# High and low meta columns side by side (288, 256 and 272 columns), with drawn places and orders for five weight tiles at a time

## The chip, the cores and the metric

The kernel runs on one core of a Trainium2 chip, in one launch. The metric is the device time of that core in microseconds. Before the change two runs gave 2329.08 and 2329.9 us, median 2329.49 us; the execution that was profiled took 2329.64 us.

## The reference

Two layers of an encoder over 272 positions (256 tokens and 16 learned meta tokens) of width 2048, float32. Cut to what matters:

```python
h = concatenate([meta, x])                       # (272, 2048)
for l in range(2):
    proj = h @ w_in[l]                           # 2048 -> 6176: GLA q,k,v,gate,decay; NA q,k,v
    y = concatenate([gla_mixer(...), na_mixer(...)])
    h = layer_norm(ALPHA * h + y @ w_out[l])     # 2048 -> 2048
    ff = square(relu(h @ w_ff1[l])) @ w_ff2[l]   # 2048 -> 8192 -> 2048
    h = layer_norm(ALPHA * h + ff)
return h[16:]                                    # the meta tokens are dropped
```

Nearly all the work is in the products with `w_in`, `w_out`, `w_ff1` and `w_ff2`, each weight read once from memory. In the second layer most outputs are needed for the 256 tokens alone.

## The kernel before

**Three products for one.** Activations lie transposed: a chunk is 128 features (partitions) by `n` positions, `n` = 272 (`L`) where the meta tokens are needed, 256 (`T`) where not. Every float32 operand is split into a high part in the TensorE's float32r type and the remainder, also float32r (`split`, `halves`). A product of float32 operands is then three float32r products: high weights by high activations ("h"), high weights by low activations ("l"), low weights by high activations ("w"). Each of them loads its 128x128 block of weights first.

**Weight tiles.** `order` lists the tiles of 128x1024 weights (8 blocks of 128 columns) in the order in which they are used, and names each one's kind. `weights` keeps two tiles made ahead: `made` issues the load of `raw` on SyncE's queue, ScalarE casts it to `wh` (L217), VectorE subtracts to get `wl` (L218). Three buffers of each rotate. The tables `HIGHS` and `LOWS` say, by kind, where in `wh` and `wl` the blocks lie: the first element, the step from an even block to the next, and the step from pair to pair, in elements of 4 bytes. Kind "all" has (0, 128, 256) and (0, 144, 320).

**Products.** `by_m` makes one output column block at a time. For each of its tiles `eight` (L252) issues 24 products in the order of `TURNS[False]`, `hlhlww` four times: two blocks by high and low activations, then their low weights. All 24 add into the same `n` columns of one PSUM bank. `by_k` (L303) makes four or eight outputs at once while activations are still being produced, with the same six products per pair of blocks. Where `n` is 256, "h" and "l" become one product of 512 columns (`once`), which needs the high and low parts as one operand; its partial sums are added in `whole`. In the second layer `sixteen` (L264) does this with all high weights of two tiles in one row and all low weights in another. Four PSUM banks ("mm") rotate between outputs. Two extra columns (274 and 258 in place of 272 and 256) carry a layer norm's gain and bias through the first products after it (`fixed`, `fix`).

**Where the parts of an activation lie.** `Pair` holds a chunk's buffer of two rows of 288 elements (2304 bytes in a partition): the high part starts at element 0, the low part at element 288. After a product an evictor (`ev_q`, `ev_f` and so on) reads the bank, and what is used as an activation again goes through `split`: a copy on ScalarE (L338) and a subtraction on VectorE (L339).

The order of the work between the products is set by generators that `pump` steps between tiles, and within an engine's queue by the order in which a scheduler lays the instructions down.

Of the kernel before, what the change touches and what calls it, by code (L numbers as in the profile page):

```python
# [2 lines left out]

# [11 lines left out]
P = 128  # L15
# [25 lines left out]
WIDE = 1280  # L41
HIGHS = {"once": (0, P, 2 * P), "two": (0, P, 2 * P), "all": (0, P, 2 * P), "all2": (0, P, 2 * P), "own2": (0, P + 48, 2 * P + 64)}
LOWS = {"once": (16, P + 32, 2 * P + 64), "two": (16, P + 16, 2 * P + 64), "all": (0, P + 16, 2 * P + 64),
        "all2": (0, P + 48, 2 * P + 64), "own2": (0, P + 32, 2 * P + 64)}
# [12 lines left out]


class Trunk:
    def __init__(self, ctx, tc, ins, out):  # L60
# [5 lines left out]
        self.stream, self.ready = self.order(), deque()  # L66
# [88 lines left out]
    def order(self):  # L155

        i, first = self.i, [(), (WB // 2, WB)]
        for l in range(DEPTH):
            last = l + 1 == DEPTH
            kind = lambda short, name: name if last and short else "all"  # L160
            na = [kind(c % 3 == 0, "two") for c in range(24)]
            groups = [(i["win"][l, g], [kind(g in (3, 4, 5), "two")] * 4 if g < 6 else na[4 * g - 24:4 * g - 20]) for g in range(12)]
# [17 lines left out]
    def weights(self):  # L180

        while len(self.ready) < 2:
            self.ready.append(self.made(*next(self.stream, (None, (), None))))
        return self.ready.popleft()

    def made(self, ap, ends, kind):
        if ap is None:
            return None
# [3 lines left out]
        wh, wl = self.blocks(wh, *HIGHS[kind]), self.blocks(wl, *LOWS[kind])  # L192
# [27 lines left out]
    def head(self, ap, raw, wh, wl):  # L220
# [7 lines left out]
        for c in range(2):  # L228
            at = slice(2 * c, 2 * c + 2)
            h, lo = (t[:, :L] for t in self.x[c])  # L230
            acts = lambda: self.split(both[:, c, q:], h, lo)
# [6 lines left out]
    def eight(self, ps, wh, wl, x, n, first, last, once):  # L238
# [4 lines left out]
        mm = self.nc.tensor.matmul  # L243
        seen = dict.fromkeys("hlw", 0)
        for i, kind in enumerate(TURNS[once]):
            j = seen[kind]
            seen[kind] += 1
            w, v, o = wl if kind == "w" else wh, x[j], ps[:, :n]
            rhs = v[kind == "l"][:, :n]
            if once:  # L250
                rhs, o = (v.once, ps) if kind == "h" else (v[0][:, :T], ps[:, T:])
            mm(o, lhsT=self.block(w, j), rhs=rhs, start=first and not i, stop=last and i == len(TURNS[once]) - 1)  # L252
# [25 lines left out]
    def by_k(self, acts, n, before, wide=False):  # L278
# [5 lines left out]
        for k in range(0, nk, 2):  # L284
# [4 lines left out]
            for g in range(0, len(ps), 4):  # L289
# [12 lines left out]
                for j, p, m in order:  # L302
                    self.nc.tensor.matmul(ps[g + m][:, :n], lhsT=self.block(parts[p][0], 4 * j + m if first else 2 * m + j), rhs=acts[k + j][parts[p][1]][:, :n],  # L303
                                          start=k + j + p == 0, stop=k == nk - 2 and j + p == 3)
        return [[p[:, :T], p[:, T:]] if n == T else [p[:, :n]] for p in ps]
# [10 lines left out]
    def by_m(self, acts, ns, evict, pump=(0, 0), apart=False, renew=False, slim=()):  # L316

        nk = len(acts)
        for m, n in enumerate(ns):
# [13 lines left out]
            parts = [ps[:, :T], ps[:, T:]] if once else [ps[:, :n]]  # L333
# [3 lines left out]
    def split(self, src, hi, lo):  # L337
        self.nc.scalar.copy(hi, src)  # L338
        self.nc.vector.tensor_tensor(lo, src, hi.bitcast(F32), ALU.subtract)  # L339

# [75 lines left out]
    def mixed(self, k):  # L416
# [3 lines left out]
        for c in (k, k + 1):  # L420
            h, lo = (t[:, :self.n].bitcast(F32) for t in self.x[c])
            self.nc.vector.tensor_tensor(self.acc[:, c, :self.n], h, lo, ALU.add)

    def load_x(self, k):
# [5 lines left out]
        for c in range(2):  # L430
            self.x[k + c] = h, lo = self.pair(self.xp, "x", k + c)
            self.split(raw[:, c, :], h[:, :L], lo[:, :L])
# [19 lines left out]
    def gates(self):  # L452
# [12 lines left out]
        for k in range(DC):  # L465
            xh, xl = self.x[k]
            for m, r in ((64, xh), (32, xl))[::-1 if k == DC - 1 else 1]:
                nc.tensor.matmul(o[:m], lhsT=ws[:, k, :m], rhs=r[:, :L], start=k == 0 and m == 64,  # L468
                                 stop=k == DC - 1 and m == 64)
# [4 lines left out]
        nc.vector.tensor_tensor(t, o[:32], t, ALU.add)  # L474
        self.stack(t, lr, 32, (0, 64), 32)
# [102 lines left out]
    def gla_head(self, h):  # L578
# [142 lines left out]
        for e in range(2):  # L721
            c = 2 * h + e
            hi, lo = (t[:, :n] for t in self.y[c])
            nc.vector.scalar_tensor_tensor(os_[e], os_[e], self.vec[:, self.l, 64 + e:65 + e], rs, ALU.mult, ALU.mult)
            self.split(os_[e], hi, lo)
# [90 lines left out]
    def na_out(self, c, v1, v2, p1, p2, pm):  # L816
# [20 lines left out]
        if self.full:  # L837
            self.split(po[0][:, P:P + NM], h[:, T:L], lo[:, T:L])
# [10 lines left out]
    def tail(self, ps):  # L849
# [3 lines left out]
        with tc.tile_pool(name="u", bufs=1, reuse_waits="tile") as up:  # L853
# [8 lines left out]
            for half in range(2):  # L862
                u = [self.pair(self.yp, "y", k) if k < DC else self.pair(up, "u", k) for k in range(2 * DC)]

                def ev_f(k, ps, **how):
                    h, lo = u[k]
# [9 lines left out]
                    self.split(t, h[:, :n], lo[:, :n])  # L876
# [71 lines left out]
    def mean(self, src, n, i=0, pool=None):  # L948

        parts = [t[:, :src.shape[-1]] for t in self.pair(pool or self.lp, "sp", i)]  # L950
# [18 lines left out]
    def ln_add(self, j, which):  # L969
        nc, n, acc = self.nc, self.n, self.acc  # L970
        d = acc[:, j, :n]
        if not which or self.l < DEPTH - 1:
            gain, bias = self.affine(self.l, which, j)
            self.x[j] = h, lo = self.pair(self.xp, "x", j)
            gb = self.vec[:, self.l, 32 * which + j:32 * which + j + DC + 1:DC]
            self.split(gb, h[:, n:n + 2], lo[:, n:n + 2])
            nc.scalar.activation(h[:, :n], d, AF.Identity, scale=gain)
            nc.vector.scalar_tensor_tensor(lo[:, :n], d, gain, h[:, :n].bitcast(F32), ALU.mult, ALU.subtract)
# [85 lines left out]
    def renew(self, end):  # L1064
# [3 lines left out]
        for c in range(f["new"], end):  # L1068
# [4 lines left out]
            h, lo = self.x[c]  # L1073
            self.split(self.acc[:, c, :n], h[:, :n], lo[:, :n])
# [9 lines left out]
    def fix(self, evict, m, ps):  # L1084
# [8 lines left out]
        nc.vector.tensor_copy(wb, ps[:, n:n + 2])  # L1093
# [160 lines left out]
```

## Time and profile before

| what | value |
|---|---|
| median of two runs | 2329.49 us |
| the profiled execution, device time | 2329.64 us |
| its span, first to last instruction | 2327.8 us |
| TensorE matmuls (PE) busy | 2318.9 us, 18052 matmuls |
| TensorE weight loads (PEld) busy | 2202.1 us, 18052 loads |
| VectorE (DVE) busy | 1522.8 us, 2440 instructions |
| ScalarE (ACT) busy | 1222.8 us, 2104 instructions |
| DMA | 179 GB/s read over the span |
| granted TensorE clock | 0.999 |

The matmuls are pipelined, so the duration of one reaches over the start of the next: at 272 columns one is recorded with some 285 ns while the next starts some 122 ns later. A busy PE is therefore read by the distance between starts, or by how the mean duration of one form differs from that of another. The first figures in a row of the grouped view are the busy time and the mean duration of one; a row of the timeline has the start, the time it spans and the count of equal instructions merged in it.

### The profile page before, as it was taken

To read this page: it belongs to the slowest core of one execution; us is meant where nothing else is said; L and a number is where in the kernel's file an instruction comes from. 1 tells how busy PE (TensorE), PEld (TensorE's weight loads), DVE (VectorE), ACT (ScalarE), POOL (GpSimd) and SP (SyncE) were. 2 spreads that over 40 slices of the span, in tenths; PEclk is the share of its full clock that TensorE was granted. 3 is DMA by queue.
4 is the path that set the end of the run, shared out by engine and by line. 5 is a ranking of instruction groups with operands and counts; after the bars stand their busy time and mean duration, and the time that the engine had idled before them with its cause. 6 is when DMAs were issued, how large, how long until landed. Compare 5 with 4: busy or idle time off the path is not lost.

```text
span 2327.8 us, 44399 instructions
## 1 busy us (share of the span) xinstructions
PE 2318.9 (100%) x18052; PEld 2202.1 (95%) x18052; DVE 1522.8 (65%) x2440; ACT 1222.8 (53%) x2104; POOL 129.4 (6%) x200
## 2 busy tenths in 40 slices
PE   9999999999999999999999999999999999999998
PEld 9999999999999999999999899989988888888888
DVE  5588777775544455547576787778866545666655
ACT  5666665564433344444456666655655334555443
POOL 0021110110000000000020111100100000000000
PEclk9999999999999999999999999999999999999999
DMA  8554545555555566655555555555666565656664
GB/s 265 155 163 155 151 146 169 173 181 181 181 178 179 179 180 182 181 179 176 181 187 165 173 168 156 158 166 186 192 198 191 190 198 190 192 198 213 199 194 150
DMA packets 118300, 419.01 MB, mean 180 GB/s; under 512 B 13512, under 2 KB 14024, under 8 KB 118096
## 3 DMA queue, kind: packets, MB, share of 16 engines
q1 hardware_dynamic: 117808, 415.65, 57.2%
q8 instruction: 141, 2.31, 0.4%
q14 instruction: 63, 0.52, 0.1%
q10 hardware_dynamic: 288, 0.52, 0.1%
HBM read 414.03 MB, written 2.10 MB: 179 GB/s over the span
## 4 chain that ended last, share of the span: by engine, by line
PE 97%; DVE 1%; issue 1%; ACT 0%; DMA 0%; POOL 0%; DVEq 0%; ACTq 0%; SPq 0%; POOLq 0%
PE mm L252 56%; PE mm L264 30%; PE mm L303 4%; PE mm L313 2%; PE bg L303 1%; PE bg L827 1%; PE mm L766 1%; DVE wl L218 0%; PE bg L627 0%; PE bg L468 0%; DVE acc L1057 0%; PE mm L792 0%; PE bg L955 0%; PE mm L516 0%; PE bg L678 0%
## 5 line engine op out<-in xcount | busy, mean ns | idle before, releaser
L218 DVE TENSOR_TENSOR wl<-raw,wh 128x1024 fp32r<-128x1024 f32 (+1 forms) x770 | 938.3, 1225 | 645.1 <-ACT wh L217 546.0
L217 ACT CAST wh<-raw 128x1024 fp32r<-128x1024 f32 (+1 forms) x770 | 805.5, 1047 | 790.5 <-PE mm L252 383.8
L252 PE MATMUL mm<-x,wh 128*128 128x272 f32 (+3 forms) x4544 | 805.7, 294 | 0.0
L252 PEld LDWEIGHTS mm<-x,wh 128*128 128x128 f32 x4544 | 646.8, 188 | 14.9 <-PE mm L766 0.6
L252 PE MATMUL mm<-x,wl 128*128 128x272 f32 (+3 forms) x2432 | 519.7, 284 | 0.0
L252 PEld LDWEIGHTS mm<-x,wl 128*128 128x128 f32 x2432 | 390.8, 188 | 0.0
L252 PE MATMUL mm<-y,wh 128*128 128x272 f32 (+1 forms) x1440 | 235.0, 285 | 0.0
L252 PEld LDWEIGHTS mm<-y,wh 128*128 128x128 f32 x1440 | 199.7, 188 | 0.1
L264 PE MATMUL mm<-x,wh 128*128 128x512 f32 x832 | 193.8, 390 | 0.0
L264 PEld LDWEIGHTS mm<-x,wh 128*128 128x128 f32 x832 | 154.3, 188 | 31.0
L252 PE MATMUL mm<-u,wh 128*128 128x272 f32 (+1 forms) x1056 | 172.1, 285 | 0.0
L264 PE MATMUL mm<-y,wh 128*128 128x512 f32 x688 | 162.3, 389 | 0.0
L264 PEld LDWEIGHTS mm<-y,wh 128*128 128x128 f32 x688 | 128.6, 188 | 26.8 <-issue 0.4
L252 PE MATMUL mm<-y,wl 128*128 128x272 f32 (+1 forms) x720 | 146.5, 285 | 0.0
L252 PEld LDWEIGHTS mm<-u,wh 128*128 128x128 f32 x1056 | 146.3, 188 | 0.0
L264 PE MATMUL mm<-u,wh 128*128 128x512 f32 x496 | 118.3, 391 | 0.0
L252 PEld LDWEIGHTS mm<-y,wl 128*128 128x128 f32 x720 | 112.6, 188 | 0.0
L264 PEld LDWEIGHTS mm<-u,wh 128*128 128x128 f32 x496 | 90.9, 188 | 17.7
L252 PE MATMUL mm<-u,wl 128*128 128x272 f32 (+1 forms) x528 | 107.3, 284 | 0.0
L264 PEld LDWEIGHTS mm<-x,wl 128*128 128x128 f32 x832 | 98.4, 188 | 2.0
L264 PE MATMUL mm<-x,wl 128*128 128x256 f32 x832 | 98.8, 276 | 0.0
L264 PEld LDWEIGHTS mm<-y,wl 128*128 128x128 f32 x688 | 84.3, 188 | 3.0 <-DVE wl L218 0.2
(286 smaller groups left out, 2297.4 us busy)
## 6 DMA issues: line engine op xcount, KB each, us to landing
raw<-in_wff SPq DMA_DIRECT2D x512, 512.0 KB, 3.6
raw<-in_win SPq DMA_DIRECT2D x190, 512.0 KB, 4.0
raw<-in_wout SPq DMA_DIRECT2D x64, 512.0 KB, 3.6
nb<-in_nab SPq DMA_DIRECT2D x16, 352.0 KB, 4.3
xraw<-in_xT SPq DMA_DIRECT2D x7, 272.0 KB, 4.5
out<-out SPq DMA_DIRECT2D x5, 256.0 KB, 3.1
brow<-in_norm SPq DMA_DIRECT2D x4, 256.0 KB, 5.1
gw<-in_wup SPq DMA_DIRECT2D x4, 196.0 KB
```

The source lines that it names most:

```text
L217: self.nc.scalar.copy(h, r)
L218: self.wl = self.nc.vector.tensor_tensor(lo, r, h.bitcast(F32), ALU.subtract).ins
L252: mm(o, lhsT=self.block(w, j), rhs=rhs, start=first and not i, stop=last and i == len(TURNS[once]) - 1)
L264: self.nc.tensor.matmul(o, lhsT=self.block(both[j // 8][low], j % 8), rhs=rhs, start=first and not i + j, stop=bool(last and i and j == 15 ...
L303: self.nc.tensor.matmul(ps[g + m][:, :n], lhsT=self.block(parts[p][0], 4 * j + m if first else 2 * m + j), rhs=acts[k + j][parts[p][1]][:, ...
L313: self.nc.tensor.matmul(o, lhsT=self.block(both[low], i), rhs=rhs, start=not low and k + i % 2 == 0, stop=k == DC - 2 and i % 2 == 1 and n ...
L766: nc.tensor.matmul(ps[hh][:, t * NKEY:t * NKEY + NKEY], lhsT=q[hs, NM + t * P:NM + t * P + P], rhs=k[hs, t, :], start=True, stop=True)
L827: nc.tensor.matmul(po[t][hs, :P], lhsT=v2[ts, hs] if rest else v1[:, t, hs], rhs=p2[ts, hh, :] if rest else p1[:, 2 * hh + t, :], start=re ...
```

## The change

- `Pair` lays a chunk out as one row of 576 elements: the low part of the 256 tokens at element 0, then the high part of all 272 positions at element 256, then the low part of the 16 meta tokens behind it (`meta`).
- "h" now runs over 288 columns (high part of 272, low part of 16 meta tokens), "l" over 256 columns (low part of the tokens), "w" over 272. Where gain and bias are carried, 274 becomes 292, 256 and 290, and 258 becomes 260, 256 and 258. The number of products and of weight loads stays.
- Columns 272 to 287 of an output's bank now hold the part of the meta tokens that comes from their low halves. `join` adds them: a copy of 16 columns on ScalarE and an addition of 16 columns on VectorE, once per output of 272 columns (188 times).
- `cut` takes the place of `split` where activations are made: the copy on ScalarE stays, the subtraction on VectorE becomes one of 256 columns and one of 16.
- For tiles of kind "all" (but the first two) `draw` picks, from a generator with a fixed seed and anew for every fifth tile, the first element and the first step of `wh` and of `wl` as multiples of 8 elements (32 bytes) below 64, the step between pairs being 320 elements, and one of three orders: `hlhlww`, `hlw hlw` or `hwl hwl`. The order is used in `eight`; in `by_k` it is not.
- Kind "two" (places (0, 128, 256) and (16, 144, 320)) is gone; its tiles take "once", (0, 128, 256) and (16, 160, 320).
- `WIDE`, the length of `wh` and `wl`, grows from 1280 to 1344 elements.

```diff
-WIDE = 1280
+WIDE = 1344
+ORDERS = "hlhlwwhlhlwwhlhlwwhlhlww", "hlwhlwhlwhlwhlwhlwhlwhlw", "hwlhwlhwlhwlhwlhwlhwlhwl"
...
-        parts = (flat[:, :T], flat[:, T:2 * T]) if dense else (both[:, 0, :], both[:, 1, :])
-        made = super().__new__(cls, parts)
-        made.dense, made.both, made.once = dense, both, flat[:, :2 * T] if dense else both[:, :, :T]
+        made = super().__new__(cls, (flat[:, T:], flat[:, :T]))
+        made.dense, made.both, made.once, made.meta = dense, both, flat[:, :2 * T], flat[:, T + L:T + L + NM]
...
+    def draw(self):
+        if self.drawn % 5 == 0:
+            r = lambda: 8 * self.dice.randrange(8)
+            self.places = (r(), P + r(), 2 * P + 64), (r(), P + r(), 2 * P + 64), ORDERS[self.dice.randrange(3)]
+        self.drawn += 1
+        return self.places
...
+        high, low, turn = self.draw() if kind == "all" and ends == (WB,) else (HIGHS[kind], LOWS[kind], TURNS[False])
+        self.turns.append(turn)
+        wh, wl = self.blocks(wh, *high), self.blocks(wl, *low)
...
-        mm = self.nc.tensor.matmul
+        mm, g = self.nc.tensor.matmul, n - T
+        wide = {"h": T + 2 * g, "l": T, "w": n + NM if g > NM else n}
         seen = dict.fromkeys("hlw", 0)
-        for i, kind in enumerate(TURNS[once]):
+        turn = TURNS[True] if once else self.turn
+        for i, kind in enumerate(turn):
...
-            w, v, o = wl if kind == "w" else wh, x[j], ps[:, :n]
-            rhs = v[kind == "l"][:, :n]
+            w, v, o = wl if kind == "w" else wh, x[j], ps[:, :wide[kind]]
+            rhs = v[kind == "l"][:, :wide[kind]]
...
+    def join(self, ps):
+        t = self.jp.tile([P, NM], F32, name="ml", tag="ml", bufs=2)
+        self.nc.scalar.copy(t, ps[:, L:L + NM])
+        self.nc.vector.tensor_tensor(ps[:, T:L], ps[:, T:L], t, ALU.add)
+        return ps[:, :L]
...
+            if n >= L:
+                self.join(ps)
...
+    def cut(self, src, pair):
+        n = src.shape[-1]
+        self.split(src, pair[0][:, :n], pair[1], T)
+        if n > T:
+            self.nc.vector.tensor_tensor(pair.meta, src[:, T:], pair[0][:, T:n].bitcast(F32), ALU.subtract)
```

TensorE, first layer, start of the first tile of the GLA gate's first output (`x_130` and `x_131` are the first two chunks of activations, `x_620` and `x_623` the last two, `mm` the output's bank); before:

```order
L252 MATMUL mm<-x_620,wl 128x272
L252 MATMUL mm<-x_623,wl 128x272
L252 MATMUL mm<-x_130,wh 128x272 x2
L252 MATMUL mm<-x_131,wh 128x272 x2
L252 MATMUL mm<-x_130,wl 128x272
L252 MATMUL mm<-x_131,wl 128x272
```

and now, where the drawn order is `hwl` (`x_634` and `x_638` are now the last two chunks):

```order
L270 MATMUL mm<-x_638,wl 128x272
L270 MATMUL mm<-x_638,wh 128x256
L270 MATMUL mm<-x_130,wh 128x288
L270 MATMUL mm<-x_130,wl 128x272
L270 MATMUL mm<-x_130,wh 128x256
L270 MATMUL mm<-x_131,wh 128x288
L270 MATMUL mm<-x_131,wl 128x272
L270 MATMUL mm<-x_131,wh 128x256
```

The six products of a pair of blocks are the same six, of 816 columns in each three as before; here the low weights stand between the two uses of the high ones.

VectorE, first layer, where outputs of the first MLP product are evicted to `u` (`ft` is the squared output, `wl` the low weights of coming tiles); before:

```order
L873 TENSOR_TENSOR ft<-ft 128x272
L339 TENSOR_TENSOR u_6143<-ft,u_6143 128x272
L218 TENSOR_TENSOR wl<-raw,wh 128x4x2x128 x2
L873 TENSOR_TENSOR ft<-ft 128x272
L339 TENSOR_TENSOR u_6144<-ft,u_6144 128x272
```

and now:

```order
L331 TENSOR_TENSOR mm<-mm,ml 128x16
L911 TENSOR_TENSOR ft<-ft 128x272
L235 TENSOR_TENSOR wl<-raw,wh 128x8x128
L370 TENSOR_TENSOR u_6393<-ft,u_6393 128x256
L376 TENSOR_TENSOR u_6393<-ft,u_6393 128x16
```

Two small instructions come to each output: the addition of `join` (L331) ahead of the eviction, and the subtraction of the meta columns (L376) behind it.

More of the change, by code (lines that the diff above doesn't have):

```diff
@@ L948, in mean @@
     def mean(self, src, n, i=0, pool=None):
-        parts = [t[:, :src.shape[-1]] for t in self.pair(pool or self.lp, "sp", i)]
+        both = (pool or self.lp).tile([P, 2, PITCH], F32R, name=f"sp{i}", tag=f"sp{i}", bufs=1)
+        parts = [both[:, v, :src.shape[-1]] for v in range(2)]
         self.split(src, *parts)
```

74 lines of the change are left out of this document (43 added, 31 removed).

## The prediction

> **What bounds the kernel now.** I read the busy shares first, then the waits of the TensorE, then the timeline of one tile, then the groups by form.
>
> ```profile
> PE 2318.9 (100%) x18052; PEld 2202.1 (95%) x18052; DVE 1522.8 (65%) x2440; ACT 1222.8 (53%) x2104; POOL 129.4 (6%) x200
> PE bg L442 <- DVE zero L439: 1.2, 1, 1.2
> PE bg L955 <- ACT sp L338: 1.0, 1, 1.0
> PE mm L303 <- DVE fx L1094: 0.7, 1, 0.7
> ```
>
> The TensorE is busy throughout and its recorded waits come to 2.9 us. Since durations of pipelined matmuls overlap, short gaps could hide behind this; but the tiles in the middle of a stage start one behind the other with a constant step, so it is the stream of products itself that sets the time:
>
> ```profile
> 300.23 0.65 PE L252 MATMUL mm<-x,wh 128*128 128x272 f32 x4
> 300.72 0.41 PE L252 MATMUL mm<-x,wl 128*128 128x272 f32 x2
> 300.96 0.65 PE L252 MATMUL mm<-x,wh 128*128 128x272 f32 x4
> 301.45 0.41 PE L252 MATMUL mm<-x,wl 128*128 128x272 f32 x2
> 301.69 0.65 PE L252 MATMUL mm<-x,wh 128*128 128x272 f32 x4
> ```
>
> Six products (hlhl, ww) take 0.73 us from start to start, 122 ns each, for 272 columns. The groups by form give the same more finely. One matmul is recorded with 285 ns where the next starts after 122, so some 163 ns of a duration is a tail that overlaps; differences between forms are differences between steps.
>
> ```profile
> L252 PE MATMUL mm<-x,wh 128*128 128x272 f32 x3584 | 588.6, 286 | 0.0
> L252 PE MATMUL mm<-x,wl 128*128 128x272 f32 x1792 | 365.1, 285 | 0.0
> L252 PE MATMUL mm<-y,wh 128*128 128x272 f32 x1408 | 229.9, 285 | 0.0
> L264 PE MATMUL mm<-x,wh 128*128 128x512 f32 x832 | 193.8, 390 | 0.0
> L264 PE MATMUL mm<-x,wl 128*128 128x256 f32 x832 | 98.8, 276 | 0.0
> L264 PE MATMUL mm<-y,wl 128*128 128x256 f32 x688 | 85.3, 277 | 0.0
> L252 PE MATMUL mm<-x,wh 128*128 128x512 f32 x320 | 112.7, 396 | 0.0
> L252 PE MATMUL mm<-x,wl 128*128 128x256 f32 x320 | 88.9, 278 | 0.0
> L252 PE MATMUL mm<-u,wh 128*128 128x256 f32 x32 | 5.1, 282 | 0.0
> L252 PE MATMUL mm<-u,wl 128*128 128x256 f32 x16 | 3.2, 281 | 0.0
> L252 PE MATMUL mm<-x,wh 128*128 128x274 f32 x384 | 63.8, 289 | 0.0
> L252 PE MATMUL mm<-x,wl 128*128 128x274 f32 x192 | 40.1, 290 | 0.0
> L252 PE MATMUL mm<-x,wh 128*128 128x258 f32 x256 | 40.8, 281 | 0.0
> L468 PE MATMUL bg<-x,ws 128*32 128x272 f32 x32 | 7.8, 287 | 0.0
> ```
>
> The reader is to see two things. First, a price per column: where products of one kind follow each other in long rows (L264), 512 columns are recorded with 390 ns and 256 with 276.5, so a column costs 113.5 / 256 = 0.443 ns. I call that line the floor; it puts 272 columns at 276.5 + 16 x 0.443 = 283.6. Second, the same width costs more elsewhere: 256 columns 281.5 in the order hlhlww (L252, the `u` rows) instead of 276.5. Nothing but the order and the places of weights and activations differs there, and each of these forms is steady over its whole group. So the products have, beside the columns, an excess that hangs on how places and orders follow each other:
>
> - tiles of kind "all", 272 columns: 285.4 over all rows at L252, 1.8 ns over the floor;
> - 274 columns (kind "all2"): floor 284.5, recorded 289.3, excess 4.8;
> - 258 columns ("own2"): floor 277.4, recorded 281, excess 3.6;
> - 256 columns in hlhlww ("once"): 5.0;
> - 512 and 256 in turn ("two"): 6 + 1.5 for two products, 3.8 each;
> - 272 columns by narrow weights (L468): 3.4.
>
> Kind "all", which holds most of the products, is thus the best of the mixed orders here, and the change replaces just its places and orders.
>
> **The change part by part.** *Columns.* Three products had 3 x 272 = 816 columns and have 288 + 256 + 272 = 816. By the floor's price that is 0. All the weight loads stay. The tiles with gain and bias go from 3 x 274 = 822 to 292 + 256 + 290 = 838: 192 such triples (384 rows of `wh`, 192 of `wl`) x 16 x 0.443 ns = 1.4 us. 258 becomes 260 + 256 + 258, the same sum.
>
> *Places and orders.* Of kind "all" there are 3008 triples at L252 and 320 at L303, 9,984 products in all (the L252 rows of x, y and u with 272 columns, and L303), some 52% of the span at 122 ns. I need their excess under the draws. No trace shows these draws. The lower bound is the floor itself, excess 0: nothing in the trace goes under it as a mean of a form. The upper bound is the worst place that a repeating pattern shows, the two low-weight products in a 274-column tile:
>
> ```profile
> 442.78 0.42 PE L252 MATMUL mm<-x,wl 128*128 128x274 f32 x2
> 443.04 0.66 PE L252 MATMUL mm<-x,wh 128*128 128x274 f32 x4
> ```
>
> They take 0.26 us, 130 ns each, where the floor has 274 x 0.443 = 121: excess 9. Between 0 and 9 I take 4.8, the upper side of the five rows above that are not "all" (3.4 to 5.0), for three reasons. A draw hardly ever gives the regular pattern of "all", where five of six weight blocks start at the same place modulo 256 bytes. The places may now be odd multiples of 32 bytes, which none in `HIGHS` and `LOWS` is. And a part of the draws (orders hlw and hwl) changes between `wh` and `wl` more often than any order at L252 with 272 columns did. Against more than 4.8 speaks that the new layout starts every high and low part at a multiple of 256 bytes (elements 0 and 256), where the low part was at 288. So the term is (4.8 - 1.8) ns x 9,984 = 30.0 us, with ends -18 us (excess 0) and +72 us (excess 9).
>
> Here a rule of the Trainium skill speaks the other way. Its page "SBUF — State Buffer", section "A bandwidth-pool intuition that's wrong (but worth ruling out)", gives the TensorE a second, independent read port for weight loads, and "SBUF: two separate sides" says that the TensorE never waits for another reader; by that, where weights lie could not cost anything. The trace does not agree, by 281.5 against 276.5 ns at 256 columns, unless all of that belongs to the order; what the sum would be by the rule is the second rival below.
>
> *Kind "two" to "once".* 40 tiles, 320 pairs, now 3.8 ns over the floor per product: between -2.4 us (none left) and about the same on the other side. I take 0.
>
> *Join and cut.* The nearest rows for 16 columns:
>
> ```profile
> L530 DVE TENSOR_SCALAR nq<-mm 128x16 f32<-128x16 f32 x8 | 1.3, 160 | 0.0
> L338 ACT CAST y<-bg 128x16 fp32r<-128x16 f32 x8 | 1.4, 172 | 7.3 <-DVE y L339 7.3
> DVE wl L218 <- ACT wh L217: 546.0, 434, 3.2
> ACT wh L217 <- PE mm L252: 383.8, 236, 3.2
> ```
>
> 188 joins cost ScalarE 188 x 0.172 = 32 us and VectorE 188 x 0.160 = 30 us; the program has 358 instructions more on VectorE, 170 of them not joins, another 27 us. On VectorE that makes 1580 of 2328 us, 68%. The last two rows show the cover: the engines that make weights wait for each other and for the TensorE to give a buffer back, hundreds of us in all, so weights are made early, not late. The output itself is ready some 0.4 us later, but four banks rotate and an output takes two tiles or more, 5.9 us, so three outputs' time lies between. Where that cover is thin is the end of the four `by_k` stages with 272 columns: there all four banks are in use to the end, and the next output needs one of them at once. The first eviction is late by one copy and one addition, 0.33 us, at each; I take 1.5 us in all, from 0 to 3.
>
> The sum against the profiled execution's own time: 2329.6 + 30.0 + 1.4 + 0 + 1.5 = 2362.5, rounded 2363 us. That execution lies 0.15 us over the median of the runs, so the sum holds for the median too. Its own range, with an excess from 3 to 6.5 and the small terms' ends, is 2342 to 2382.
>
> **The rivals.** *The layout locks in.* High and low parts now start at multiples of 256 bytes, and 288 and 256 columns are whole multiples of 128 bytes, so the stream of activations goes on from "h" to "l" without a step. Long rows of such products at L264 have no excess. If the activations' steps cause the excess and not the weights', it falls to some 0.5: -1.3 x 9,984 = -13.0 us, with 2.9 for the rest 2319.5 us, faster than before. It decides below an excess of 1.5, where the gain outweighs the 2.9. Against it: the 256-column hlhlww tiles also have whole multiples and starts at 0 and 256, and 5 ns. Chance 0.12.
>
> *Places don't matter.* What differs between the forms is something else (the width, the target bank), the 1.8 stays, and only columns and joins count: 2329.6 + 2.9 = 2332.5 us. By the Trainium skill's page "SBUF — State Buffer" (above) this is what the change would do. The 512-column rows speak against it, 396 with other neighbours, 390 in rows. Chance 0.10.
>
> *The draws clash like the worst pair.* With 32-byte offsets and a change of weights before each product the excess is 7.8: 6.0 x 9,984 = 59.9, so 2392 us. It decides from 6.2 on, where 2% (46.6 us) is passed. For it: the low-weight pairs of a 274-column tile come near it; against it: no whole form does. Chance 0.17.
>
> *The joins end up on the path.* If VectorE, waiting for `join`'s copy behind ScalarE's casts, delays weights each time, 188 x 0.33 = 62 us come on top of 1.4: 2393 us without any cost of places. The waits quoted above say that both have time to spare. Chance 0.06.
>
> **How the numbers follow.** The forecast has 0.55, the rivals 0.12, 0.10, 0.17 and 0.06. The range, 2322 to 2390 us, leaves out the first rival and about half of the slow ones. A measurement of this kernel can tell about 2% from no change, here 2283 to 2376 us. Slower by over 2%: the two slow rivals and the upper edge of the forecast, 0.23 + 0.03 = 0.26. Faster by over 2% would need more than twice what the floor allows: 0.02. Within 2%: 0.72.
>
> **What would show it.** In the profile after, the matmuls of 288, 256 and 272 columns at L270 should have means of 295.5, 281.3 and 288.4 ns (floor plus 4.8); the tail of 163 ns should be unchanged. Means should differ from one group of five tiles to the next, with steps of six products from 0.72 to 0.79 us. PE's waits should stay at a few us, DVE near 68%. The forecast is wrong if the three means lie at the floor (290.7, 276.5, 283.6), if they lie 7 or more above it, or if PE shows waits for VectorE or ScalarE of tens of us.

## The result, and the profile after

| what | before | after |
|---|---|---|
| median of two runs, us | 2329.49 | 2367.02 (2366.92 to 2367.11) |
| span of the profiled execution, us | 2327.8 | 2365.1 |
| matmuls busy, us | 2318.9 | 2353.7 |
| VectorE busy, us | 1522.8 | 1557.7 |
| ScalarE busy, us | 1222.8 | 1244.8 |

The changed kernel takes 1.0163 of the time before (interval 1.0138 to 1.0187): 37.5 us slower, 1.6%. The forecast was 2363 us, within 2% and slower.

From the page of after, the span and the busy shares, and from its waits all those of the TensorE of 0.4 us or more (engine, line waited at, releaser: us in total, times, longest):

```profile
span 2365.1 us, 45038 instructions
PE 2353.7 (100%) x18052; PEld 2232.3 (94%) x18052; DVE 1557.7 (66%) x2798; ACT 1244.8 (53%) x2312; POOL 118.1 (5%) x200
PE bg L481 <- DVE zero L478: 1.2, 1, 1.2
PE mm L340 <- ACT x L367: 1.1, 1, 1.1
PE mm L323 <- DVE x L376: 1.1, 1, 1.1
PE mm L323 <- DVE nr L579: 0.4, 1, 0.4
```

All of the TensorE's waits come to 5.4 us, where they were 2.9. The 37 us are therefore not in waits: the same 18052 matmuls take longer from start to start. The groups by form show it (the two figures between the bars are the busy time in us and the mean duration in ns of one):

```profile
L270 PE MATMUL mm<-x,wh 128*128 128x288 f32 x1792 | 513.6, 297 | 0.3 <-ACT ft L543 0.3
L270 PE MATMUL mm<-y,wh 128*128 128x288 f32 x704 | 202.5, 295 | 0.0
L270 PE MATMUL mm<-x,wh 128*128 128x256 f32 x2112 | 574.4, 280 | 0.0
L270 PE MATMUL mm<-y,wh 128*128 128x256 f32 x736 | 199.1, 281 | 0.0
L270 PE MATMUL mm<-x,wl 128*128 128x272 f32 x1792 | 450.5, 288 | 0.0
L270 PE MATMUL mm<-y,wl 128*128 128x272 f32 x704 | 182.5, 288 | 0.0
```

288, 256 and 272 columns are recorded with 295 to 297, 280 to 281 and 288 ns. A set of three is some 864 ns where three products of 272 columns had 286, 286 and 285, 857 ns. And in the timeline, in a group of five tiles that drew the order of before:

```profile
634.16 0.42 PE L270 MATMUL mm<-x,wl 128*128 128x272 f32 x2
634.42 0.67 PE L270 MATMUL mm<-x,wh 128*128 128x288 f32 x4
634.92 0.42 PE L270 MATMUL mm<-x,wl 128*128 128x272 f32 x2
635.18 0.67 PE L270 MATMUL mm<-x,wh 128*128 128x288 f32 x4
635.68 0.42 PE L270 MATMUL mm<-x,wl 128*128 128x272 f32 x2
```

Six products took 0.73 us before; here they take 0.76 us (634.42 to 635.18).

**The account.** I took the distance from each matmul's start to the next in both traces and summed it over the same products (in `by_k` distances of 400 ns and more are left to the last row, the waits):

| where | before, us | after, us | difference |
|---|---|---|---|
| kind "all" at L252, now L270 (8,969 distances) | 1100.7 (122.72 ns each) | 1126.5 (125.60) | +25.8 |
| kind "all" in `by_k` (some 955) | 124.65 ns each | 126.4 | +1.7 |
| gain and bias, 274 columns (574) | 72.4 | 74.0 | +1.6 |
| gain and bias, 258 columns | 45.6 | 45.1 | -0.5 |
| 512 and 256 in turn, "two", now "once" (630) | 110.7 | 112.2 | +1.5 |
| `sixteen`, L264, now L283 | 688.1 | 692.0 | +3.9 |
| the TensorE's recorded waits | 2.9 | 5.4 | +2.5 |

That is 36.5 of the 37.3 us of the span; the rest is in small products.

### The profile page after: what moved, and what is told of

It is laid out like the page before. It is cut to its first block, busy times and chain, and to the rows that moved or that the text cites. A ratio compares the mean times of both kernels' runs of the same rounds, so it can differ in the third digit from the quotient of the medians.

```text
span 2365.1 us, 45038 instructions
## 1 busy us (share of the span) xinstructions
PE 2353.7 (100%) x18052; PEld 2232.3 (94%) x18052; DVE 1557.7 (66%) x2798; ACT 1244.8 (53%) x2312; POOL 118.1 (5%) x200
## 4 chain that ended last, share of the span: by engine, by line
PE 97%; DVE 2%; ACT 1%; issue 0%; DVEq 0%; ACTq 0%
PE mm L270 57%; PE mm L283 29%; PE mm L323 4%; PE mm L340 2%; PE bg L323 1%; PE bg L866 1%; DVE wl L235 1%; PE bg L667 0%; PE mm L805 0%; PE bg L507 0%; DVE acc L1098 0%; ACT wh L234 0%; PE mm L831 0%; PE bg L994 0%; PE mm L556 0%
## 5 line engine op out<-in xcount | busy, mean ns | idle before, releaser
L234 ACT CAST wh<-raw 128x1024 fp32r<-128x1024 f32 (+1 forms) x770 | 805.7, 1047 | 720.0 <-PE mm L270 261.6
L270 PE MATMUL mm<-x,wh 128*128 128x288 f32 (+3 forms) x4544 | 863.2, 296 | 0.3 <-ACT ft L543 0.3
L270 PEld LDWEIGHTS mm<-x,wh 128*128 128x128 f32 x4544 | 687.8, 188 | 16.1 <-PE mm L805 0.6
L270 PE MATMUL mm<-x,wl 128*128 128x272 f32 (+3 forms) x2432 | 606.8, 287 | 0.0
L270 PEld LDWEIGHTS mm<-x,wl 128*128 128x128 f32 x2432 | 418.6, 188 | 0.0
L270 PE MATMUL mm<-y,wh 128*128 128x256 f32 (+1 forms) x1440 | 261.4, 288 | 0.0
L270 PEld LDWEIGHTS mm<-y,wh 128*128 128x128 f32 x1440 | 218.1, 188 | 0.1
L270 PE MATMUL mm<-u,wh 128*128 128x256 f32 (+1 forms) x1056 | 194.2, 288 | 0.0
L283 PE MATMUL mm<-x,wh 128*128 128x512 f32 x832 | 193.8, 390 | 0.0
L270 PE MATMUL mm<-y,wl 128*128 128x272 f32 (+1 forms) x720 | 185.7, 288 | 0.0
L283 PEld LDWEIGHTS mm<-x,wh 128*128 128x128 f32 x832 | 154.3, 188 | 31.1
L283 PE MATMUL mm<-y,wh 128*128 128x512 f32 x688 | 163.8, 391 | 0.0
L270 PEld LDWEIGHTS mm<-u,wh 128*128 128x128 f32 x1056 | 161.6, 188 | 0.0
L283 PEld LDWEIGHTS mm<-y,wh 128*128 128x128 f32 x688 | 128.6, 188 | 28.5 <-issue 0.4
L270 PE MATMUL mm<-u,wl 128*128 128x272 f32 (+1 forms) x528 | 140.7, 287 | 0.0
L270 PEld LDWEIGHTS mm<-y,wl 128*128 128x128 f32 x720 | 126.5, 188 | 0.0
L283 PE MATMUL mm<-u,wh 128*128 128x512 f32 x496 | 120.0, 394 | 0.0
L283 PEld LDWEIGHTS mm<-u,wh 128*128 128x128 f32 x496 | 91.2, 188 | 19.0
L283 PEld LDWEIGHTS mm<-x,wl 128*128 128x128 f32 x832 | 98.6, 188 | 2.2
L283 PE MATMUL mm<-x,wl 128*128 128x256 f32 x832 | 99.2, 277 | 0.0
L270 PEld LDWEIGHTS mm<-u,wl 128*128 128x128 f32 x528 | 94.6, 188 | 0.0
```

The costliest lines, as they stand in the source:

```text
L234: self.nc.scalar.copy(h, r)
L283: self.nc.tensor.matmul(o, lhsT=self.block(both[j // 8][low], j % 8), rhs=rhs, start=first and not i + j, stop=bool(last and i and j == 15 ...
```

## The experiments

"Step" below is the mean distance between starts in the middle 12 of a tile's 24 products, in ns, averaged over the 372 tiles of kind "all" in `eight`; 122.45 before, 125.28 after. All medians are in us, ratios against the kernel before on the same chip.

The expectations name theories by letters. A, the prediction's own: the drawn places cost it, the layout is neutral. Its rivals put the cost (B) on the layout, or (C) on the drawn orders. In the edits below "..." stands for lines of an edit that are not shown.

**The layout without the draws.**

```diff
-            self.places = (r(), P + r(), 2 * P + 64), (r(), P + r(), 2 * P + 64), ORDERS[self.dice.randrange(3)]
+            self.places = HIGHS["all"], LOWS["all"], ORDERS[0]
```

> The change with its layout and its 288, 256 and 272 columns, but every tile of kind all takes the places of before, (0, 128, 256) and (0, 144, 320), and the order hlhlww. Theory A (the drawn places cost, the layout is neutral): the mean step of a product in these tiles falls back from 125.3 to about 122.5 ns, the time to 2330 to 2340 us. Theory B (the layout of the activations with unequal widths costs): the step stays near 125, the time at 2358 to 2367. Theory C (the orders hlw and hwl cost): as A.

Measured 2373.05, ratio 1.0185 (1.0168 to 1.0202), step 125.94. The whole group of 288 columns, with the weights where they lay before:

```profile
L270 PE MATMUL mm<-x,wh 128*128 128x288 f32 x1792 | 494.4, 298 | 0.1
```

The layout without the draws costs 43 us, more than the change with its draws. On the places of before the layout is not neutral, so that premise of the prediction fell as it stood.

**The draws without the layout.** `draw` and the orders are put into the kernel before, with `WIDE` 1344; layout, joins and kind "two" stay.

```diff
...
-        wh, wl = self.blocks(wh, *HIGHS[kind]), self.blocks(wl, *LOWS[kind])
+        high, low, turn = self.draw() if kind == "all" and ends == (WB,) else (HIGHS[kind], LOWS[kind], TURNS[False])
+        self.turns.append(turn)
+        wh, wl = self.blocks(wh, *high), self.blocks(wl, *low)
...
-        for i, kind in enumerate(TURNS[once]):
+        turn = TURNS[True] if once else self.turn
+        for i, kind in enumerate(turn):
...
```

> The kernel before with nothing but the drawn places and orders of the change; layout, equal widths of 272 columns and evictions as before. Theory A: nearly all of the loss without the layout, step 125 ns, 2353 to 2363 us. Theory B: close to before, 2328 to 2338 us. If the new layout softens the clashes (the low parts now start at a multiple of 256 bytes), this kernel is slower than the change, over 2367 us.

Measured 2358.11, ratio 1.0122 (1.0107 to 1.0137), step 125.33.

```profile
L267 PE MATMUL mm<-x,wh 128*128 128x272 f32 x3584 | 644.0, 288 | 0.0
L267 PE MATMUL mm<-y,wh 128*128 128x272 f32 x1408 | 256.3, 288 | 0.0
```

286 and 285 became 288: the draws alone cost 28 us with every column count and start of before. So 43 for the one, 28 for the other, and 37.5 for both together. These are not two costs that add up; they look like two ways out of one good setting. The traces show it in the tiles themselves: the starts of the products of kind "all" in `eight` are 31.8 us further apart in sum with the layout, 25.8 with the draws, and 25.8 with both. So on drawn places the layout costs these tiles nothing more. The other 11 to 12 us of the two kernels with the layout lie in the rest of the account above; of the draws alone that rest is 2.7 us.

**Draws of places alone, and of orders alone, in the changed kernel.** The first keeps `hlhlww`, the second the places of before:

```diff
+            self.places = self.places[:2] + (ORDERS[0],)
```
```diff
+            self.places = HIGHS["all"], LOWS["all"], self.places[2]
```

Both edits keep the draws of the generator and then replace the orders or the places.

> The change with all its drawn places, but always in the order hlhlww. Theory A: steps as in the tiles that had this order by draw, mean 125.3 ns against 125.3 over all, so 2363 to 2368 us. Theory C: about 2345 us.

> The change with its drawn orders, but the places of before, (0, 128, 256) and (0, 144, 320), in every tile of kind all. Theory A: 2332 to 2345 us, a little over the layout alone, since hwl changes between high and low weights more often. Theory C: over 2350 us.

Measured 2367.01 (ratio 1.0165, 1.0149 to 1.018; step 125.25) and 2370.72 (1.0177, 1.0162 to 1.0192; step 125.67). The first is the change's own time, so on drawn places the orders give nothing and take nothing: C falls. In the changed kernel itself, tiles with `hlhlww`, `hlw` and `hwl` have mean steps of 125.2, 125.1 and 125.5. The second was expected far lower, and missed because with this layout the places of before are no better than drawn ones. On this one set of places the order does count: in the second kernel the three orders have 126.2, 125.1 and 125.6.

**Widths or starts?** Two theories of what the layout costs: W, that its unequal widths do it; S, that the new starts of the activations do it. One kernel keeps all of before and shortens "l" to 256 columns (the low part of the meta tokens is left out); the other takes the changed kernel's starts and places of before, but 272 columns for all three products in `eight` ("l" then takes 16 columns of the high part along, the meta columns hold other values, and `by_m` has no join for these outputs).

```diff
-            w, v, o = wl if kind == "w" else wh, x[j], ps[:, :n]
-            rhs = v[kind == "l"][:, :n]
+            m = T if kind == "l" and n == L else n
+            w, v, o = wl if kind == "w" else wh, x[j], ps[:, :m]
+            rhs = v[kind == "l"][:, :m]
...
```
```diff
+            self.places = HIGHS["all"], LOWS["all"], ORDERS[0]
...
+        wide = {"h": T + 2 * g, "l": T, "w": n + NM if g > NM else n} if n != L else dict.fromkeys("hlw", L)
...
+            rhs = (v.both.rearrange("p a c -> p (a c)") if kind == "l" else v[0])[:, :wide[kind]]
...
+            if n > L:
```

> The kernel before, layout, places and order as they were, but "l" at L252 runs over 256 columns in place of 272 (the low part of the meta tokens is left out), so that the widths in a tile are unequal: 272, 256, 272. By the floor's price that takes 3008 x 16 x 0.443 ns = 21.3 us away. Theory W (unequal widths break the pattern): the excess per product rises from 1.9 to 4 or 5 ns, time 2327 to 2337 us. Theory S (the starts of the new layout do it): excess stays at 1.9, time 2308 us.

> The layout of the change with the places and the order of before, as in the run with the layout alone, but in the tiles of 272 columns h, l and w all run over 272 columns, each from the new starts ("l" takes 16 columns of the high part along in place of the low meta columns; no join there, the meta tokens' values are off). Theory W: the steps of before come back, 122 to 123 ns, time 2332 to 2340 us. Theory S: steps stay at 125 to 127 ns as with the layout alone, time 2360 to 2372 us.

The first measured 2328.05, ratio 0.9994 (0.9985 to 1.0003), the second 2374.29, 1.0192 (1.0178 to 1.0206). The first kernel's groups, and its timeline:

```profile
L253 PE MATMUL mm<-x,wh 128*128 128x272 f32 x1792 | 478.8, 290 | 0.0
L253 PE MATMUL mm<-x,wh 128*128 128x256 f32 x1792 | 470.1, 280 | 0.0
L253 PE MATMUL mm<-x,wl 128*128 128x272 f32 x1792 | 367.2, 286 | 0.0
```
```profile
300.36 0.66 PE L253 MATMUL mm<-x,wh 128*128 128x272 f32 x4
300.85 0.41 PE L253 MATMUL mm<-x,wl 128*128 128x272 f32 x2
301.10 0.65 PE L253 MATMUL mm<-x,wh 128*128 128x272 f32 x4
301.59 0.41 PE L253 MATMUL mm<-x,wl 128*128 128x272 f32 x2
301.83 0.65 PE L253 MATMUL mm<-x,wh 128*128 128x272 f32 x4
```

32 columns fewer in six products (14 ns at 0.443 ns a column), and six products still take 0.735 us (300.36 to 301.83 is two of them). What the 256-column product saved against 272 (280 instead of 286), its 272-column neighbours lost (290 instead of 286). Here the time follows something other than columns, as W said; 2308 us, what the columns alone would give, fell. The group of the second kernel says the reverse of the starts:

```profile
L270 PE MATMUL mm<-x,wh 128*128 128x272 f32 x3584 | 600.9, 290 | 0.0
L270 PE MATMUL mm<-x,wl 128*128 128x272 f32 x1792 | 370.3, 287 | 0.0
```

The same product of the same width, with the weights at the same places, takes 290 with the activations' halves at 256 and 0 and took 286 with them at 0 and 288. Equal widths don't bring it back; the starts are enough by themselves. Against the step of before (122.45), unequal widths at the old starts change nothing (122.24), and the new starts with equal widths make 126.26. So in these tiles it is the starts that make the layout's cost; W is right only in that the columns saved bring no time.

**The join left out.** `join` returns the bank without the copy, the addition and the tile `ml`; the 16 columns are then not added to the meta tokens.

> The change with all it draws, but the join left out (the 16 columns from the low halves are not added; its two small tiles go too, so that the later activation buffers u start at a multiple of 256 bytes again). If joins lie off the path: 0 to 3 us less than the change, 2364 to 2367 us; the 512-column rows of u, 394 ns in the change, tell apart what the moved buffers cost (back to 391 if the place does it, 1 to 4 us in all). If joins are on the path: up to 62 us less.

Measured 2366.96, ratio 1.0159 (1.0145 to 1.0173), 0.06 us from the changed kernel. That the joins cost up to 62 us fell; a cost of a few us could hide, since two things in its trace cancel. One wait has grown, and the rows of 512 columns at L283 have fallen; the kernel without the join first:

```profile
PE mm L323 <- ACT x L364: 4.3, 1, 4.3
L283 PE MATMUL mm<-x,wh 128*128 128x512 f32 x832 | 193.8, 390 | 0.0
L283 PE MATMUL mm<-y,wh 128*128 128x512 f32 x688 | 162.3, 389 | 0.0
L283 PE MATMUL mm<-u,wh 128*128 128x512 f32 x496 | 118.3, 390 | 0.0
```

then the changed kernel:

```profile
L283 PE MATMUL mm<-x,wh 128*128 128x512 f32 x832 | 193.8, 390 | 0.0
L283 PE MATMUL mm<-y,wh 128*128 128x512 f32 x688 | 163.8, 391 | 0.0
L283 PE MATMUL mm<-u,wh 128*128 128x512 f32 x496 | 120.0, 394 | 0.0
```

The order, the weights' places and the columns of these rows are the same in both. What differs is where the buffers of `u` begin: the two buffers of `ml`, 64 bytes each, lie ahead of them, and move every start of `u` to 128 bytes off a multiple of 256. The joins' own instructions can't be the reason: in the changed kernel the last one is done at 1552 us, and the first of these rows starts at 1578. From start to start a product of 512 columns on `u` takes 231.9 ns in the changed kernel and 228.3 without the joins, so 495 of them 1.8 us. The buffers of `y` lie at the same addresses in both, and yet 229.1 became 227.0, another 1.4 us. The changed kernel's timeline shows which rows of `y` make this:

```profile
1822.90 3.79 PE L283 MATMUL mm<-y,wh 128*128 128x512 f32 x16
...
1830.18 3.87 PE L283 MATMUL mm<-u,wh 128*128 128x512 f32 x16
1833.89 3.84 PE L283 MATMUL mm<-y,wh 128*128 128x512 f32 x16
```

The first row on `y`, with no row on `u` before it, steps (3.79 - 0.39) / 15 = 226.7 ns (0.39 us is the record of its last product), as without the joins. The next one follows directly on a row on `u`, and steps 230.0. So it goes in both stretches in which rows on `y` and `u` take turns: 28 of the 29 rows on `y` that follow a row on `u` have 230.0, and the first row of either stretch has 226.7. A row's step thus hangs on the row before it, too. Some 37 us over the kernel before stay without joins.

**Are there better places?** Three surveys give each group of five tiles another pair of offsets, all 64 combinations in one kernel, order `hlhlww`: the low weights' first element and first step in the kernel before (high weights at 0, 128, 320), the same in the changed kernel, and the first steps of high and low weights in the kernel before.

```diff
+            k = self.drawn // 5 % 64
+            self.places = (0, P, 2 * P + 64), (8 * (k // 8), P + 8 * (k % 8), 2 * P + 64), ORDERS[0]
```
```diff
+            self.places = (0, P + 8 * (k // 8), 2 * P + 64), (0, P + 8 * (k % 8), 2 * P + 64), ORDERS[0]
```

> The kernel before, order hlhlww, high weights at (0, 128, 320), low weights at (c, 128 + d, 320) for c and d from 0 to 56 in steps of 8, a pair of places for every five tiles. The regular high weights of before are kept, and only the low ones move. If one irregular block more or less is enough to lose the pattern, the 64 steps spread from 122 to 127 ns with (0, 16), before's own, among the best; if the low weights hardly matter, they all lie within a nanosecond of 122.3. As a whole 2340 to 2355 us.

> The change with a survey in place of the draws: order hlhlww, high weights at (0, 128, 320), low weights at (c, 128 + d, 320), c and d from 0 to 56 in steps of 8, five tiles each. Theory: good combinations are rare in any layout, one or two in a hundred; so 0 to 3 of the 64 come to 122.3 ns a product or under, most lie between 124.4 and 127. If the new layout itself can't lock, none is under 124. As a whole 2363 to 2372 us.

> The kernel before, order hlhlww, high weights at (0, 128 + e, 320), low weights at (0, 128 + d, 320), e and d from 0 to 56 in steps of 8, five tiles each. The same theory: e = 0, d = 16 (before's places) at 122.3 ns, and at most a few others there; a mean step under 122 ns would be a kernel faster than before. As a whole 2350 to 2360 us.

They took 2355.5, 2369.8 and 2356.47 us in one run each. What counts are the steps by combination (the median of its tiles). In the first, two combinations of those that occur have 122.2: first element 0 with a first step of 128 + 16, which is before's own, and 32 with 128 + 40; the others lie between 123.3 and 126.7. In the second none is under 123.3, and most are at 124.4 to 127.8. In the third 122.2 occurs only where before has it. Nothing in any of them is under 122.

The totals of six products tell more than their means. Most of them bunch on a ladder 6.7 ns apart; the table counts the 372 tiles by the nearest rung (a pattern may need 12 products to repeat, and then its mean can stand half a rung off):

| six products, ns | 733.5 | 740 | 747 | 753.5 | 760 | 767 |
|---|---|---|---|---|---|---|
| before | 340 | 2 | 18 | 12 | 0 | 0 |
| after | 0 | 8 | 148 | 167 | 48 | 1 |
| layout alone | 0 | 0 | 61 | 152 | 159 | 0 |
| draws alone | 0 | 12 | 146 | 160 | 45 | 9 |
| layout, equal widths | 0 | 0 | 28 | 79 | 265 | 0 |
| before, "l" shortened | 363 | 9 | 0 | 0 | 0 | 0 |
| survey of low weights, before | 11 | 42 | 88 | 195 | 36 | 0 |
| survey of low weights, after | 0 | 5 | 86 | 212 | 58 | 11 |
| survey of first steps, before | 6 | 14 | 142 | 166 | 43 | 1 |

Before's tiles sit on the lowest rung, nearly all of them. Every departure in the places of weights or the starts of activations lands two to four rungs up on average; a rung is 6.7 / 6 = 1.1 ns per product, so that is 2.2 to 4.5 ns. The shortened "l" stays where before is (its totals are about 732 and 734).

**The best places among the change's own draws, in all tiles.**

```diff
-            self.places = (r(), P + r(), 2 * P + 64), (r(), P + r(), 2 * P + 64), ORDERS[self.dice.randrange(3)]
+            self.places = (16, P + 8, 2 * P + 64), (40, P, 2 * P + 64), ORDERS[0]
```

> The change with the best places that its own draws showed, (16, 136, 320) and (40, 128, 320) in the order hlhlww, in every tile of kind all. If the step of a tile follows from its places, widths and layout alone: 123.3 ns a product in all these tiles, 1.9 ns less than the draws' mean, so 2367 - 9,500 x 0.0019 = 2349 us. If the step of that draw hung on where in the program it fell: no change beyond 2360 us.

Measured 2360.13, ratio 1.0128 (1.0111 to 1.0145): 7 us better than the change, 11 us short of what was expected, 30 us over the kernel before.

```profile
L270 PE MATMUL mm<-x,wh 128*128 128x288 f32 x1792 | 490.5, 296 | 0.1
L270 PE MATMUL mm<-y,wh 128*128 128x288 f32 x704 | 190.6, 293 | 0.0
L270 PE MATMUL mm<-u,wh 128*128 128x288 f32 x512 | 139.8, 295 | 0.0
```

One form, one set of places, three means. 84 of the 86 tiles on `y` have the 123.3 that a draw had shown; all 64 on `u`, whose buffers start 128 bytes off, have 125.6; and of 222 on `x` 127 have 123.3, while 94 have about 126, with the same widths, order, places of weights and starts of activations modulo 256 bytes. The trace shows when they change: of the 168 tiles on `x` that follow directly on another, 167 keep the step of the one before (96 at 123.3, 71 at 126), and none goes from one of the two to the other. Where a change between them comes, other products lie between the tiles. With the layout alone it is the same with three steps (125.0, 125.6 and 126.7), which 167 of 168 such tiles keep. In the kernel before, the 14 such tiles whose predecessor had another step are all back at 122.2. So a setting can have several steps that sustain themselves, and the row's entry picks one; before's falls back into its lowest. What at the entry picks the step is not shown.

**Regularity taken apart.** In the kernel before, groups of five tiles take turns in eight variants: one weight block for all products (1), the high part's start for all activations (2), 256 columns (4), and their sums. It leaves out parts of the product, so only its steps are read.

```diff
+            m = T if v8 & 4 and not (first and not i) else n
+            o, rhs = ps[:, :m], v[kind == "l" and not v8 & 2][:, :m]
+            mm(o, lhsT=self.block(wh, 0) if v8 & 1 else self.block(w, j), rhs=rhs, start=first and not i,
...
```

> The kernel before, order and places as they were, in eight variants that follow each other every five tiles of kind all. Bit 1: all products load block 0 of the high weights (the other blocks are left out). Bit 2: "l" reads the high part too, so that all activations start at a multiple of 256 bytes (the low part is left out). Bit 4: all products but a group's first run over 256 columns (16 columns are left out). Variant 0 is before, 122.3 ns a product (floor 120.4 at 272, 113.3 at 256 columns). If changes of the weights' places make the excess: variants 1, 3, 5, 7 lie at the floor within 0.5 ns, the others 2 to 6 ns over it. If the streams' starts and lengths make it: variants 6 and 7, with whole multiples of 128 bytes and one start, lie at the floor, the others over it. If only both together give the floor: variant 7 alone.

| variant | none | 1 | 2 | 1+2 | 4 | 4+1 | 4+2 | all |
|---|---|---|---|---|---|---|---|---|
| step, ns (median of 41 to 50 tiles) | 122.25 | 124.4 | 125.4 | 125.3 | 118.9 | 118.8 | 119.0 | 120.0 |

None of the three outcomes that were named came. The time of this kernel was 2322.53 us in one run. The timeline of it has a tile of variant 1+2, one of "all", and a row of `sixteen`:

```profile
628.84 3.17 PE L268 MATMUL mm<-y,wh 128*128 128x272 f32 x24
...
686.67 3.04 PE L268 MATMUL mm<-y,wh 128*128 128x256 f32 x24
```
```profile
1708.95 3.80 PE L281 MATMUL mm<-x,wl 128*128 128x256 f32 x32
```

The 24 products of 256 columns have one weight block and one start: (3.04 - 0.28) / 23 = 120.0 ns each. The 32 of `sixteen`, with another block each, take (3.80 - 0.28) / 31 = 113.5. The difference is 6.5 ns in every product. The two rows differ in more than the blocks (`sixteen` writes to the other half of the bank, and its weights lie at other places), but within this kernel, too, the most regular of the 256-column patterns is the dearest, 120.0 against 118.8 to 119.0. That before was quick because its pattern is regular fell too: at 272 columns one block and one start make 125.3 of 122.25. The variant "none" also shows that the longer `wh` and `wl` (`WIDE` 1344), which this kernel has, don't move the step of before.

## Why the prediction was right, and where its reasons were not

**What bounds the kernel.** Right: the TensorE's stream before and after, waits of 5.4 us, VectorE at 66% where 68% was forecast.

**Columns.** The sum was kept for the gain and bias tiles: 1.6 us measured, 1.4 forecast. As a price that can be taken off anywhere, the 0.443 ns fell: 32 columns less in six brought nothing in the shortened kernel. It holds between long rows of `sixteen`, from which it was read. And those rows are no floor of columns alone, since the rows on `u` stand 4 ns higher where their buffers are shifted.

**Places and orders.** The term was 30.0 us; it measured 25.8 + 1.7 = 27.5. The forecast excess of 4.8 ns became 5.0 (125.60 at L270 against 120.6, the 113.5 ns by which 256 columns follow each other in `sixteen` and 16 x 0.443); its starting value was 2.1 by the same measure, not 1.8, so the rise is 2.9 where 3.0 was forecast. The three means came out at 295 to 297, 280 to 281 and 288, against 295.5, 281.3 and 288.4, and six products take 0.74 to 0.76 us by group of five, where 0.72 to 0.79 was forecast. That the draws are what costs here is shown: without the layout they cost the same tiles the same 25.8 us. But 4.8 was a choice between 0 and 9, and the reasons for it did not hold, so that it came so near is in part luck. Perhaps the rows it was read from, 3.4 to 5.0, are what a setting costs that isn't the best one; no run tests that.

Of the three reasons one half holds. Regularity: a draw does hardly ever reach the step of "all" (no tile of the change or of the draws alone is on the lowest rung), but it isn't regularity that makes this step, since the pattern with one block and one start is dearer. Odd multiples of 32 bytes: of the survey's four lowest settings three have one (first step 128 + 40 twice, 128 + 56 once), in that survey tiles with none and with two of them both average 125.2, and the places of before, with none, gave 125.94 in the new layout. Changes between `wh` and `wl`: on drawn places the three orders differ by 0.4 ns, and on the places of before `hlhlww`, which changes least, is the dearest. And the reason that I gave against a higher value, starts at multiples of 256 bytes, is a cost where the places of before are kept (31.8 us in these tiles), and nothing on drawn ones. The prediction put the whole term down to the draws; in the new layout, the kernel would have been slower still without them. There the draws replaced one bad setting by a mean over bad ones.

**"Two" to "once".** Forecast 0, within 2.4 either way; +1.5 us.

**Joins.** Forecast 1.5, from 0 to 3. The TensorE's waits rose by 2.5 us, but no more than 0.06 us went when the joins were taken out, since a wait of 4.3 us came in another place; so their own cost is not shown more closely than a few us. Their cover held: ScalarE's weights still wait for the TensorE to return a buffer, 261.6 us in the trace of after, as in this row:

```profile
ACT wh L234 <- PE mm L270: 261.6, 198, 2.8
```

**Not foreseen.** 3.9 us in `sixteen`, whose code the change leaves alone. 3.2 of it go when `join` and its buffers do: 1.8 on the `u` that they shift by 128 bytes, and 1.4 on the rows of `y` that follow them. With `once` and the waits that is 7.9 us against the 1.5 that I had for joins, and 2.5 less in the large term; so 2363 stood 4 us under 2367, with errors of both signs in it.

**The rivals.** *The layout locks in*: it does the reverse, 125.94 with the places of before, and in its whole survey nothing under 123.3. *Places don't matter*: fell by the draws alone, 28 us with the same widths and starts, and by the surveys, where in one order the weights' places alone make 122.2 to 126.7 ns. The prediction had set the Trainium skill's page "SBUF — State Buffer" behind this rival: weight loads have a read port of their own ("A bandwidth-pool intuition that's wrong (but worth ruling out)"), and the TensorE waits for no one ("SBUF: two separate sides"). The trace doesn't agree that a block's place is free, by these 122.2 against 126.7 ns; whether the port is the reason, no run shows. *The worst pair*: only 1 of 372 tiles reaches the top rung. *Joins on the path*: 0.06 us.

**What stays open.** Shown: a product's step depends jointly on the places of the weights, the starts of the activations and the order, and within one setting on what ran before; most totals of six products stand 6.7 ns apart; before's setting is on the lowest rung that any run found at 272 columns. Not shown: what collides. My reading is that a weight load and the stream of activations, whose records overlap, meet at the same part of memory at times that the preceding products set. That a step is kept from tile to tile, and passes from rows on `u` to rows on `y`, fits that; no run tested it. Nor did any find a version with the full product that beats the kernel before.

## What to carry to other kernels

Where a stream of matmuls bounds a kernel, the places of weights, the starts of activations, the widths and the order are one setting, and they are measured together: adding the measured cost of one edit to that of another gives 71 us here where both together cost 37.5. Several dozen settings fit into one run, five tiles each, read by distances between starts; when the present setting is already the lowest of them, a first forecast for an edit of places or starts, for whatever good reason, is the mean of the others. Before adding a small buffer, look at what is allocated behind it: two buffers of 64 bytes here shifted others, and a stage whose code the change didn't touch became 3 us dearer.

## What the hardware showed that I had not expected

- Most totals of six products with 1632 columns in all stand on rungs 6.7 ns apart (733.5, 740, 747, 753.5, 760, 767), and 24 equal products of 256 columns step 120.0 ns where 32 with different blocks step 113.5.
- 32 columns fewer in six products changed nothing: 0.735 us for six, ratio 0.9994 (0.9985 to 1.0003). The neighbours' records grew from 286 to 290 ns as the shortened one's fell to 280.
- One setting had two steps, 123.3 and about 126 ns, in tiles of one form in one kernel, and 167 of 168 tiles that followed directly on another kept the step of that one.
- Products of 512 columns went from 390 to 394 ns (`u`) where their activations' buffers lay 128 bytes further, and from 389 to 391 (`y`) where nothing of them was moved, but rows on `u` ran before them (230.0 ns from start to start against 226.7).
